# Output units of a feed-forward layer: quarter results subtracted on VectorE instead of GpSimd, six tiles split in the following stage, and a table of angles built in five parts

## The chip, the cores and the metric

One NeuronCore of a Trainium2 chip runs the whole program as a single launch. The metric is device time in microseconds (us). The core has five engines with a queue each: TensorE for matrix products (PE in the profile; PEld is its loading of stationary operands), VectorE (DVE), ScalarE (ACT), GpSimd (POOL) and SyncE (SP), which here only issues DMAs. Each engine works through its own queue in order; engines wait for one another through semaphores.

## What is computed

A trunk of two layers over 512 tokens and a width of 1024, all in float32. Layer 0 mixes tokens with a Conformer convolution module, layer 1 with a sparse attention (NSA). Each is followed by a SwiGLU feed-forward layer with 2816 hidden units:

```python
def swiglu_ffn(h, w_in, w_out):
    gate, up = jnp.split(h @ w_in, 2, axis=-1)
    return (jax.nn.silu(gate) * up) @ w_out

for i in range(DEPTH):
    h = rmsnorm(x, norm_mix[i])
    x = x + (conformer_conv_module(h, ...) if i == 0 else nsa_attention(h, positions, ...))
    h = rmsnorm(x, norm_ffn[i])
    x = x + swiglu_ffn(h, ffn_w_in[i], ffn_w_out[i])
```

The attention rotates part of each query and key by an angle that depends on the position; the kernel needs the cosines and sines of these angles as two tables.

## The kernel before

The residual x lies transposed in eight tiles x[0] to x[7] of 128 channels by 512 tokens. Every operand of a product is split into a rounded part and a remainder (`wh`, `wl` for weights, `hh`, `hl` for the normed x, `sh`, `sl` for sums of weights): ScalarE writes the rounded part, VectorE subtracts it from the value to get the remainder, and TensorE makes three matmuls in place of one (high by high, high by low, low by high).

The program runs through these stages in order of time: convolution module, feed-forward layer 0, attention, feed-forward layer 1. The end of a feed-forward layer (function `ffn`, from line 801) is what the change is about. It multiplies the hidden units by `w_out` in two ways:

- **Row stage.** Fourteen of the 22 hidden blocks are taken one at a time (the loop over `j` with `start(j)`, lines 1090 to 1106). Each row is 24 matmuls of 512 columns into eight PSUM banks. At each row ScalarE and VectorE also split the weights of the next row (`w_hi`, `w_lo`) and the hidden block of a later one (`row_part`, by the table `ROW_AT`). Beside that, in rows 2 to 6 they prepare the operands of the next stage: `raw_blocks` splits three quarter-blocks of two hidden tiles and then forms four differences and sums of quarters in place, with `nc.gpsimd.tensor_tensor` (line 1059); `sum_blocks` splits those. In layer 0, row 7 also calls `between()`, which builds the whole angle table (`rope_tables`, line 1190): a DMA of the positions, ten VectorE operations, three ScalarE operations, two more on VectorE. At the end the eight banks are added to x.
- **Output units.** The other eight hidden blocks go through four units (`out_pair`, line 1131), each of which gives two output tiles m0 and m1 by a scheme with seven products of half-size blocks in place of eight. A product is 12 matmuls of 256 columns (four chunks of the contraction, three matmuls each). TensorE's order in a unit is: weights (into bank a), part ga (bank d), the previous unit's last product (`out_tail`), ga again (a), weights again (b), gb (d), gb (a). Copies of intermediate results (c1, c5, c2) are made by ScalarE; `take_half` subtracts such a copy from a half of an x tile on GpSimd, `add_half` adds a PSUM bank to a half on VectorE. GpSimd also forms the sums of weights that the next unit needs (`s_add`, two operations) and issues the DMAs `s_pre` and `s_acc`; `s_part` (in `s_g1`, `s_g2` and for gc) splits these sums.

When an x tile of layer 0 is complete, `give` calls `finish_x`: `split_x` makes `hh[m]` (ScalarE) and `hl[m]` (VectorE) for the attention's projections, and `sum_x` squares the tile on ScalarE and adds it to the accumulator `acc` of the RMS norm, on VectorE for odd m and on GpSimd for even m. In a unit this stands between `add_half(m0, 1, ...)` and `add_half(m1, 1, ...)`. In layer 1 there is no next stage and `give` stores the tile to the output instead.

The attention begins with `proj_start` (line 395): eight steps k, each with 12 matmuls of 512 columns that use `hh[k]` and `hl[k]`. Functions hooked to a step are called behind it; before, `norm_1` (sum over channels by TensorE, then a reciprocal square root on VectorE) stands behind step 2, `norm_2` (broadcast by TensorE, copy by ScalarE) behind step 3.

The order of the work is written by hand: instructions wrapped in `pe(...)` or `held(...)`, and all of them while `order[0]` is true, keep their place in the program order of their engine. Others are placed by the compiler's scheduler. Nearly all instructions go through the wrapper `Ordered`, so the profile gives line 149 for them; they are told apart by the names of their tiles.

Of the kernel before, what the change touches and what calls it, by code (L numbers as in the profile page):

```python
# [19 lines left out]
P = 128  # L20
T = 512
# [49 lines left out]

QV_ORDER = (0, 1, 2, 3, 4, 5, 6, 7, 8, 9)
VW = (304, 256)
NSA_HOOKS = ("", "", "a", "b", "", "", "", "lc")
BESIDE = {
# [34 lines left out]
NR = len(RROWS)  # L110
NOUT = NK // 2
NALL = NST + NOUT
ROW_SLOT = {11: "gah", 12: "gal", 13: "S2", 14: "gbh", 15: "gah", 16: "gal", 17: "S2", 18: "gbh", 19: "S2", 20: "gbh", 21: "gbl"}
ROW_AT = {1: (21, 11), 2: (12,), 3: (13,), 4: (14,), 5: (15,), 6: (16,), 7: (17,), 8: (18,), 10: (19,), 11: (20,)}
RAW_AT = {2: 0, 3: 1, 4: 2, 5: 3}
SUM_AT = {3: 0, 4: 1, 5: 2, 6: 3}
TABLES_AT = 7
ROW_ORDER = {0: (0, 1, 2, 3, 4), NR - 1: (0, 1, 2, 7, 5, 6, 3, 4)}
OUT_N = 256
EDGE = 24  # L120
# [41 lines left out]
def trunk(ctx: ExitStack, tc: tile.TileContext, A, out):  # L162
# [11 lines left out]
    def nm(s):  # L174
        cnt[0] += 1
        return f"{s}_{cnt[0]}"
# [186 lines left out]
    def finish_x(m, gcol, acc, eng=None):  # L363
        split_x(m, gcol)
        sum_x(m, acc, eng)
# [435 lines left out]
    def ffn(acc, gnext, layer, between=None):  # L801
# [9 lines left out]
        with ExitStack() as cx:  # L811
# [96 lines left out]
            def s_add(n):  # L908
                if n < NALL:
                    w = raws[u0 + n + (NR if n >= NST else 0)]  # L910
                    t = S2[n] = sw.tile([P, 2 * T], F32, tag="S2", name=nm("S2"))
                    pe(nc.gpsimd.tensor_tensor(t[:, :T], S[n][:, :T], w[:, :T], ALU.add))
                    pe(nc.gpsimd.tensor_tensor(t[:, T:], t[:, :T], w[:, T:2 * T], ALU.add))
# [120 lines left out]
                rh[f] = ah[f], al[f]  # L1034

            def row_part(f):
                t = sw.tile([P, 2 * T], F32R, tag=ROW_SLOT[f], name=nm("row"))
                rh[f] = h_, l_ = t[:, :T], t[:, T:]
# [12 lines left out]
            def raw_blocks(c):  # L1051
                y1, y2 = ys[SROWS[c]], ys[SROWS[c + 4]]
                block(c, slice(0, H), y1[:, :H], True)
                block(c, slice(H, 3 * H), y2)
                for z, a, b, o in ((y1[:, :H], y1[:, :H], y1[:, H:], ALU.subtract),
                                   (y1[:, H:], y1[:, H:], y2[:, H:], ALU.subtract),
                                   (y2[:, H:], y1[:, :H], y2[:, H:], ALU.add),
                                   (y2[:, :H], y2[:, :H], y2[:, H:], ALU.subtract)):
                    pe(nc.gpsimd.tensor_tensor(z, a, b, o))

            def sum_blocks(c):
                block(c, slice(3 * H, 5 * H), ys[SROWS[c]])
                block(c, slice(5 * H, 7 * H), ys[SROWS[c + 4]])
# [26 lines left out]
            for j in range(1, NR):  # L1090
                start(j)
                for f in ROW_AT.get(j, ()):
                    row_part(f)
                if j in RAW_AT:
                    raw_blocks(RAW_AT[j])
                if j in SUM_AT:
                    sum_blocks(SUM_AT[j])
                if j == NR - 2:
                    s_add(NST)
                if j == NR - 1:  # L1100
                    s_g1(NST)
                if j == TABLES_AT and layer == 0:
                    hold[0], order[0] = False, True
                    between()
                    hold[0], order[0] = True, False
                row_mm(j, ROW_ORDER.get(j, range(NK)))
            for m in ROW_ORDER[NR - 1]:
# [6 lines left out]

            def take_half(m, h, t):
                z = x[m][:, h * H:(h + 1) * H]
                pe(nc.gpsimd.tensor_tensor(z, z, t, ALU.subtract))

            def give(m, h=None):
                if gnext is None:  # L1120
                    c = slice(0, T) if h is None else slice(h * H, (h + 1) * H)
                    nc.sync.dma_start(out[m][:, c], x[m][:, c])
                elif h is None:
                    hold[0], order[0] = False, True
                    finish_x(m, gnext, acc, nc.vector if m % 2 else nc.gpsimd)
                    hold[0], order[0] = True, False

            def out_tail(q):
# [2 lines left out]
            def out_pair(n, prev):  # L1131
                m0 = 2 * (n - NST)
                m1 = m0 + 1
                end = n == NALL - 1
                q = dict(n=n, a=bank(), m1=m1)
                w1 = next_w(False)
                product(q["a"], w1, 0, 0, True, True)
                s_g2(n)
                s_acc(n + 2)
                s_pre(n + 3)  # L1140
                s_add(n + 1)
                s_load(n + 2)
# [12 lines left out]
                s_part(n, "gc", raw[n])  # L1155
                b = bank()
                product(b, w1, 1, 1, True, True)
                take_half(m0, 1, copied(q["a"], "c2"))
                s_g1(n + 1)
                if end:  # L1160
                    product(q["a"], part[n, "gb"], 0, 4, False, True)
                    add_half(m1, 1, q["a"])
                    give(m1, 1)
                product(q["d"], part[n, "gb"], 1, 2, False, True)
                add_half(m0, 0, b)
                if end:
                    give(m0, 0)
# [3 lines left out]
                if end and gnext is None:  # L1171
                    give(m0, 1)
# [8 lines left out]
                q = out_pair(n, q)  # L1181
            out_tail(q)
            add_half(q["m1"], 0, q["a"])
            give(q["m1"], 0) if gnext is None else give(q["m1"])
            hold[0] = False
            sx.close()
        return acc
# [2 lines left out]
    def rope_tables():  # L1190
        rp = hx[0].enter_context(tc.tile_pool(name="rp", bufs=1))
        cosT = rp.tile([P, T], F32, name="cosT")
        sinT = rp.tile([P, T], F32, name="sinT")
        pos = tp.tile([P, T], I32, tag="sq", name="pos")
        nc.gpsimd.dma_start(pos, A["positions"].partition_broadcast(P))
        pf = tp.tile([P, T], F32, tag="sq", name="posf")
        n = tp.tile([P, T], F32, tag="sq", name="ropen")
        g = nc.vector
        g.tensor_copy(pf, pos)
        g.tensor_scalar(pf, pf, v(V_INVF), None, ALU.mult)  # L1200
        big = 1.5 * 2.0 ** 23
        g.tensor_scalar(n, pf, 1.0 / (2.0 * math.pi), big, ALU.mult, ALU.add)
        g.tensor_scalar(n, n, -big, None, ALU.add)
        for c in _two_pi_pieces():
            g.scalar_tensor_tensor(pf, n, -c, pf, ALU.mult, ALU.add)
        lim = 3.1415925
        g.tensor_scalar(pf, pf, lim, -lim, ALU.min, ALU.max)
        nc.scalar.activation(sinT, pf, AF.Sin)
        nc.scalar.activation(n, pf, AF.Abs)
        nc.scalar.activation(cosT, n, AF.Sin, bias=halfpi, scale=-1.0)  # L1210
        g.tensor_scalar(sinT, sinT, v(V_SGN), None, ALU.mult)
        g.tensor_scalar(cosT, cosT, v(V_ISR), v(V_NISR), ALU.mult, ALU.add)
        return cosT, sinT


    def nsa(acc, cosT, sinT, gnext):
# [112 lines left out]
            box["R"] = norm_b(box["r"], p2, "p2")  # L1329

        def nsa_hooks():
            f = {"l": loads, "c": C["split"], "a": norm_1, "b": norm_2}
            hs = {}
# [614 lines left out]
    acc = conv_module()  # L1948
    cx0.close()
    rope = []  # L1950
    acc = ffn(acc, V_NM1, 0, lambda: rope.extend(rope_tables()))
    cosT, sinT = rope
    acc = nsa(acc, cosT, sinT, V_NF1)
    ffn(acc, None, 1)
    hx[0].close()
# [164 lines left out]
```

## Time and profile before

| | |
|---|---|
| median of 3 runs | 1193.58 us (1193.27 to 1194.09) |
| the profiled execution, its own time | 1193.79 us |
| its span, first to last instruction | 1192.0 us |
| mean granted TensorE clock | 0.997 |
| busy: PE, DVE, ACT, POOL | 1166.9, 870.8, 589.2, 459.9 us |
| row stage of layer 0, output units of layer 0 | about 412 to 485 us, 485 to 535 us of the span |
| start of the attention's projections | from 535 us |
| output units of layer 1 | 1149 us to the end |

The page gives the busy time of each engine and groups instructions by line, operation and tiles. A row of the timeline has the start in us, the duration, the engine, the operation with output tile and input tiles, the count, and in square brackets the idle time before it and what ended it. A row of a group has the count, the busy time in us, the mean of one instruction in ns, and idle time before it with what ended it. A row of the windows has, for a stretch of the span, the busy time of PE, PEld, DVE, ACT and POOL (with counts), the granted clock of TensorE and DMA figures. Ends of matmuls are modelled, so a short wait between two matmuls can be hidden under the modelled end of the first.

### The profile page before, as it was taken

What the parts mean: (1) busy time and instruction counts of PE and PEld (TensorE: products, weight loads), DVE (VectorE), ACT (ScalarE), POOL (GpSimd) and SP (SyncE); (2) the same over time, 40 slices, a digit from 0 to 9 for tenths busy, and PEclk for the clock granted to TensorE, in tenths of its full rate; (3) what the DMA queues carried; (4) which work ended last, traced back from release to release, by engine and by line L of the source; (5) the groups of instructions that cost most, each with busy time, mean ns of one, the idle gap of its engine ahead of it and who ended that gap; (6) DMA issues with size and microseconds to landing.
All of it is one profiled execution on the core that took longest, in us unless ns stands there. A gap on an engine that the chain in (4) does not pass through costs nothing.

```text
span 1192.0 us, 21615 instructions
## 1 busy us (share of the span) xinstructions
PE 1166.9 (98%) x8303; PEld 1018.2 (85%) x8303; DVE 870.8 (73%) x1526; ACT 589.2 (49%) x1118; POOL 459.9 (39%) x484
## 2 busy tenths in 40 slices
PE   9999899999999999989999999999999999999998
PEld 7888678899999987888778877777888999998888
DVE  7989696878777585784678788774497887766566
ACT  6212363455555452453434688783354555545343
POOL 1039022135444160543222468661303544433245
PEclk9999999999999999999999999999999999999999
DMA  9735326357777522424354211111534877772333
GB/s 365 259 109 143 81 89 194 103 163 203 187 194 203 153 100 93 115 80 117 109 133 123 71 37 37 36 37 56 182 112 129 198 200 189 196 201 89 105 103 94
DMA packets 84440, 160.60 MB, mean 135 GB/s; under 512 B 36336, under 2 KB 37488, under 8 KB 83568
## 3 DMA queue, kind: packets, MB, share of 16 engines
q1 hardware_dynamic: 65664, 106.95, 29.0%
q0 software_dynamic: 18672, 52.27, 18.6%
q8 instruction: 65, 1.06, 0.4%
q14 instruction: 39, 0.32, 0.1%
HBM read 145.66 MB, written 5.28 MB: 127 GB/s over the span
## 4 chain that ended last, share of the span: by engine, by line
PE 51%; DVE 4%; issue 3%; POOL 2%; ACT 2%; DVEq 0%; POOLq 0%; ACTq 0%
PE st L149 23%; PE pp L149 15%; PE O L149 3%; PE S L149 3%; PE T L149 3%; PE pv L149 2%; POOL S L149 1%; DVE sl L149 1%; ACT Pm L149 1%; DVE Pm L149 1%; POOL x L149 1%; DVE x L149 1%; PE psc L149 0%; PE z L149 0%; PE psq L149 0%
## 5 line engine op out<-in xcount | busy, mean ns | idle before, releaser
L149 PE MATMUL st<-ball,sh 128*128 128x256 f32 x1680 | 294.3, 277 | 6.7 <-DVE x L149 6.2
L149 PEld LDWEIGHTS st<-ball,sh 128*128 128x128 f32 x1680 | 255.4, 189 | 8.1 <-DVE x L149 7.3
L149 ACT ACTIVATE wh<-wr 128x1024 fp32r<-128x1024 f32 (+3 forms) x146 | 151.1, 1035 | 205.8 <-PE st L149 72.6
L149 DVE TENSOR_TENSOR wl<-wr,wh 128x1024 fp32r<-128x1024 f32 (+3 forms) x146 | 182.5, 1250 | 79.3 <-ACT wh L149 77.0
L149 PE MATMUL st<-ball,sl 128*128 128x256 f32 x840 | 232.9, 277 | 1.7 <-DVE sl L149 1.7
L149 POOL TENSOR_TENSOR S<-S,wr 128x512 f32<-128x512 f32 x84 | 121.6, 1448 | 140.3 <-PE st L149 58.4
L149 PE MATMUL pp<-hh,wh 128*128 128x512 f32 x416 | 165.4, 398 | 1.7 <-ACT wh L149 1.0
L149 PE MATMUL pp<-hl,wh 128*128 128x512 f32 x416 | 162.2, 390 | 0.0
L149 PE MATMUL pp<-hh,wl 128*128 128x512 f32 x416 | 162.0, 390 | 0.1
L149 PEld LDWEIGHTS st<-ball,sl 128*128 128x128 f32 x840 | 159.1, 189 | 2.3 <-DVE sl L149 2.3
L149 POOL DMA_DIRECT2D S<-fw_x x84 | 74.7, 889 | 208.6 <-DVE sl L149 157.3
L149 DVE TENSOR_TENSOR sl<-S,sh 128x512 fp32r<-128x512 f32 x168 | 118.9, 750 | 29.0 <-ACT sh L149 29.0
L149 PE MATMUL st<-ball,wh 128*128 128x256 f32 x672 | 118.7, 276 | 0.0
L149 PE MATMUL st<-row,wh 128*128 128x512 f32 x352 | 108.5, 389 | 0.9 <-ACT wh L149 0.9
L149 POOL TENSOR_SCALAR Pm<-Pm,sm,gates 128x512 f32<-128x512 f32 (+3 forms) x128 | 83.3, 663 | 55.2 <-DVE sm L149 33.7
L149 PEld LDWEIGHTS st<-ball,wh 128*128 128x128 f32 x672 | 101.7, 188 | 0.3
L149 ACT ACTIVATE sh<-S 128x512 fp32r<-128x512 f32 x168 | 96.0, 620 | 7.8 <-PE st L149 6.9
L149 PEld LDWEIGHTS pp<-hh,wh 128*128 128x128 f32 x416 | 78.2, 188 | 22.6 <-issue 3.7
L149 PEld LDWEIGHTS pp<-hh,wl 128*128 128x128 f32 x416 | 78.1, 188 | 17.2 <-DVE wl L149 0.6
L149 PE MATMUL st<-ball,wl 128*128 128x256 f32 x336 | 92.6, 276 | 0.0
L149 PEld LDWEIGHTS pp<-hl,wh 128*128 128x128 f32 x416 | 78.2, 188 | 15.8 <-issue 0.2
L149 ACT ACTIVATE Pm<-Pm,mx 128x512 f32<-128x512 f32 (+3 forms) x128 | 70.7, 554 | 29.9 <-DVE mx L149 27.1
(263 smaller groups left out, 2207.2 us busy)
## 6 DMA issues: line engine op xcount, KB each, us to landing
S<-fw_x POOLq DMA_DIRECT2D x84, 512.0 KB, 6.0
wr<-fw_in SPq DMA_DIRECT2D x46, 512.0 KB
wr<-fw_or SPq DMA_DIRECT2D x28, 512.0 KB
r<-fw_x SPq DMA_DIRECT2D x42, 256.0 KB
bd<-bands POOLq DMA_DIRECT2D x6, 1280.0 KB, 18.4
wr<-cw_in SPq DMA_DIRECT2D x14, 512.0 KB
wr<-fw_s SPq DMA_DIRECT2D x8, 512.0 KB
wr<-fw_op SPq DMA_DIRECT2D x8, 512.0 KB
```

Source lines behind the costliest of these rows:

```text
L149: z = f(*a, **kw)
```

## The change

Six edits, of which the first four apply to both layers:

1. `take_half` and the four in-place differences of `raw_blocks` run on VectorE instead of GpSimd.
2. `raw_blocks` and `sum_blocks` are spread over rows 2 to 9 instead of 2 to 6, and the hidden blocks use other buffers, so that the first unit's sums can be made one row earlier: `s_add(NST)` behind row 11, `s_g1(NST)` behind row 12, and `s_g2(NST)` behind row 13 instead of inside the first unit.
3. In a unit, `w_hi` and `w_lo` of the next weights move ahead of the previous unit's tail; the copy c5 is taken before, and subtracted after, the additions of the previous unit; `s_g1` of the next unit comes ahead of the subtraction of c2.
4. `give` is cut in two: `store` (layer 1) stays where it was.
5. In layer 0 only x[0] and x[1] are finished in the units (in the second and the third unit, both sums on GpSimd). The tiles x[2] to x[7] are split and squared behind steps 0 to 5 of `proj_start` (`LATE`), whose instructions now all keep program order; `norm_1` moves behind step 5 and `norm_2` behind step 6.
6. The angle table is built in five parts behind rows 8 to 12: load, turns (four VectorE operations), rest (six), sines (three ScalarE operations), scaled (two).

```diff
-NSA_HOOKS = ("", "", "a", "b", "", "", "", "lc")
+NSA_HOOKS = ("2", "3", "4", "5", "6", "7a", "b", "lc")
+LATE = {2: (2, 2), 3: (3, 3, 4), 4: (4, 5), 5: (5, 6), 6: (6, 7), 7: (7,)}
...
-ROW_SLOT = {11: "gah", 12: "gal", 13: "S2", 14: "gbh", 15: "gah", 16: "gal", 17: "S2", 18: "gbh", 19: "S2", 20: "gbh", 21: "gbl"}
-ROW_AT = {1: (21, 11), 2: (12,), 3: (13,), 4: (14,), 5: (15,), 6: (16,), 7: (17,), 8: (18,), 10: (19,), 11: (20,)}
-RAW_AT = {2: 0, 3: 1, 4: 2, 5: 3}
-SUM_AT = {3: 0, 4: 1, 5: 2, 6: 3}
-TABLES_AT = 7
+ROW_SLOT = {11: "gah", 12: "gal", 13: "S2", 14: "gbh", 15: "gbl", 16: "gah", 17: "gal", 18: "S2", 19: "gbh", 20: "gbl"}
+ROW_AT = {1: (21, 11), 2: (12,), 3: (13,), 4: (14,), 5: (15,), 6: (16,), 7: (17,), 8: (18,), 9: (19,), 10: (20,)}
+RAW_AT = {2: 0, 4: 1, 6: 2, 8: 3}
+SUM_AT = {3: 0, 5: 1, 7: 2, 9: 3}
+FINISHED = 2
+TABLES_AT = {8: 0, 9: 1, 10: 2, 11: 3, 12: 4}
...
-                    pe(nc.gpsimd.tensor_tensor(z, a, b, o))
+                    pe(nc.vector.tensor_tensor(z, a, b, o))
...
+                if j == NR - 3:
+                    s_add(NST)
                 if j == NR - 2:
-                    s_add(NST)
+                    s_g1(NST)
                 if j == NR - 1:
-                    s_g1(NST)
-                if j == TABLES_AT and layer == 0:
+                    s_g2(NST)
+                if j in TABLES_AT and layer == 0:
                     hold[0], order[0] = False, True
-                    between()
+                    between(TABLES_AT[j])
...
-                pe(nc.gpsimd.tensor_tensor(z, z, t, ALU.subtract))
+                pe(nc.vector.tensor_tensor(z, z, t, ALU.subtract))
...
-                    finish_x(m, gnext, acc, nc.vector if m % 2 else nc.gpsimd)
+                    finish_x(m, gnext, acc, nc.gpsimd)
...
-                s_g2(n)
+                if n > NST:
+                    s_g2(n)
...
                 take_half(m0, 0, copied(q["a"], "c1"))
+                w_hi(state["next"])
+                w_lo()
                 if prev:
                     out_tail(prev)
-                take_half(m1, 1, copied(q["d"], "c5"))
+                c5 = copied(q["d"], "c5")
                 if prev:
                     add_half(prev["m1"], 0, prev["a"])
-                    give(prev["m1"])
-                w_hi(state["next"])
-                w_lo()
+                    store(prev["m1"])
+                    if n <= NST + FINISHED:
+                        give(n - NST - 1)
+                take_half(m1, 1, c5)
...
-                take_half(m0, 1, copied(q["a"], "c2"))
+                c2 = copied(q["a"], "c2")
                 s_g1(n + 1)
+                take_half(m0, 1, c2)
...
                 add_half(m0, 1, q["d"])
...
                 else:
-                    give(m0)
-                if not end:
+                    store(m0)
                     add_half(m1, 1, q["a"])
...
         def nsa_hooks():
+            def late(m, *sums):
+                split_x(m, V_NM1)
+                for i in sums:
+                    sum_x(i, acc, nc.vector if i % 2 else nc.gpsimd)
...
+        order[0] = True
         pss = proj_start(px, "px", hh, hl, nsa_hooks())
+        order[0] = False
```

`rope_tables` is cut into the five functions `load`, `turns`, `rest`, `sines` and `scaled`, with the same operations in the same order.

More of the change, by code (lines that the diff above doesn't have):

```diff
@@ L1036, in row_part @@
             def row_part(f):
-                t = sw.tile([P, 2 * T], F32R, tag=ROW_SLOT[f], name=nm("row"))
-                rh[f] = h_, l_ = t[:, :T], t[:, T:]
+                if f in ROW_SLOT:
+                    t = sw.tile([P, 2 * T], F32R, tag=ROW_SLOT[f], name=nm("row"))
+                    rh[f] = h_, l_ = t[:, :T], t[:, T:]
+                else:
+                    rh[f] = h_, l_ = [sw.tile([P, T], F32R, tag="gc" + e, name=nm("row")) for e in "hl"]
                 pe(nc.scalar.activation(h_, ys[f], AF.Copy))
@@ L1116, in take_half, with store @@
                 z = x[m][:, h * H:(h + 1) * H]
-                pe(nc.gpsimd.tensor_tensor(z, z, t, ALU.subtract))
-            def give(m, h=None):
+                pe(nc.vector.tensor_tensor(z, z, t, ALU.subtract))
+            def store(m, h=None):
                 if gnext is None:
@@ L1122, in give @@
                     nc.sync.dma_start(out[m][:, c], x[m][:, c])
-                elif h is None:
+            def give(m):
+                if gnext is not None:
                     hold[0], order[0] = False, True
-                    finish_x(m, gnext, acc, nc.vector if m % 2 else nc.gpsimd)
+                    finish_x(m, gnext, acc, nc.gpsimd)
                     hold[0], order[0] = True, False
@@ L1162, in out_pair @@
                     add_half(m1, 1, q["a"])
-                    give(m1, 1)
+                    store(m1, 1)
                 product(q["d"], part[n, "gb"], 1, 2, False, True)
@@ L1166, in out_pair @@
                 if end:
-                    give(m0, 0)
+                    store(m0, 0)
                 else:
@@ L1170, in out_pair @@
                 add_half(m0, 1, q["d"])
-                if end and gnext is None:
-                    give(m0, 1)
-                else:
-                    give(m0)
-                if not end:
+                if end:
+                    store(m0, 1)
+                else:
+                    store(m0)
                     add_half(m1, 1, q["a"])
@@ L1183, in ffn @@
             add_half(q["m1"], 0, q["a"])
-            give(q["m1"], 0) if gnext is None else give(q["m1"])
+            store(q["m1"], 0)
             hold[0] = False
@@ L1193, in rope_tables @@
         sinT = rp.tile([P, T], F32, name="sinT")
[L1194 to L1197, printed above, removed]
         g = nc.vector
[L1199 to L1212, printed above, removed]
@@ L1213, in rope_tables, with load, turns @@
-        return cosT, sinT
+        z = {}
+        def load():
+            z["pos"] = tp.tile([P, T], I32, tag="sq", name="pos")
+            nc.gpsimd.dma_start(z["pos"], A["positions"].partition_broadcast(P))
+        def turns():
+            pf = z["pf"] = tp.tile([P, T], F32, tag="sq", name="posf")
+            n = z["n"] = tp.tile([P, T], F32, tag="sq", name="ropen")
+            g.tensor_copy(pf, z["pos"])
+            g.tensor_scalar(pf, pf, v(V_INVF), None, ALU.mult)
+            big = 1.5 * 2.0 ** 23
+            g.tensor_scalar(n, pf, 1.0 / (2.0 * math.pi), big, ALU.mult, ALU.add)
+            g.tensor_scalar(n, n, -big, None, ALU.add)
@@ new lines, in rest, with sines @@
+        def rest():
+            pf, n = z["pf"], z["n"]
+            for c in _two_pi_pieces():
+                g.scalar_tensor_tensor(pf, n, -c, pf, ALU.mult, ALU.add)
+            lim = 3.1415925
+            g.tensor_scalar(pf, pf, lim, -lim, ALU.min, ALU.max)
+        def sines():
+            pf, n = z["pf"], z["n"]
+            nc.scalar.activation(sinT, pf, AF.Sin)
+            nc.scalar.activation(n, pf, AF.Abs)
+            nc.scalar.activation(cosT, n, AF.Sin, bias=halfpi, scale=-1.0)
@@ L1216, in nsa, with scaled @@
+        def scaled():
+            g.tensor_scalar(sinT, sinT, v(V_SGN), None, ALU.mult)
+            g.tensor_scalar(cosT, cosT, v(V_ISR), v(V_NISR), ALU.mult, ALU.add)
+        return cosT, sinT, (load, turns, rest, sines, scaled)
     def nsa(acc, cosT, sinT, gnext):
@@ L1331, in nsa_hooks @@
         def nsa_hooks():
+            def late(m, *sums):
+                split_x(m, V_NM1)
+                for i in sums:
+                    sum_x(i, acc, nc.vector if i % 2 else nc.gpsimd)
             f = {"l": loads, "c": C["split"], "a": norm_1, "b": norm_2}
+            for k, z in LATE.items():
+                f[str(k)] = lambda z=z: late(*z)
             hs = {}
@@ L1950, in trunk, with tables @@
     rope = []
-    acc = ffn(acc, V_NM1, 0, lambda: rope.extend(rope_tables()))
-    cosT, sinT = rope
+    def tables(i):
+        if not rope:
+            rope.extend(rope_tables())
+        rope[2][i]()
+    acc = ffn(acc, V_NM1, 0, tables)
+    cosT, sinT = rope[:2]
     acc = nsa(acc, cosT, sinT, V_NF1)
```

## The prediction

> **What bounds the kernel now.** I read the page first, then the waits of TensorE, then its timeline and the granted clock at the two ends of feed-forward layers, then the chain of waits there, and last the groups of these stretches.
>
> ```profile
> span 1192.0 us, 21615 instructions
> PE 1166.9 (98%) x8303; PEld 1018.2 (85%) x8303; DVE 870.8 (73%) x1526; ACT 589.2 (49%) x1118; POOL 459.9 (39%) x484
> ```
>
> TensorE is the bound: no edit here removes a matmul, so all that can be won is time in which it waits or runs slowly. In its timeline, the output units of layer 0 run from the first row here to the last:
>
> ```profile
> 485.50 0.39 PE L149 MATMUL st<-ball,wh 128*128 128x256 f32 x2
> ...
> 499.24 0.50 PE L149 MATMUL st<-ball,sh 128*128 128x256 f32 x2 [2.66 <-DVE x L149]
> ...
> 512.31 0.39 PE L149 MATMUL st<-ball,sh 128*128 128x256 f32 x2
> ...
> 516.39 0.39 PE L149 MATMUL st<-ball,sh 128*128 128x256 f32 x2
> ...
> 535.19 0.39 PE L149 MATMUL pp<-hh,wh 128*128 128x512 f32 x1
> ```
>
> Between the third and fourth of them lie 12 groups of three matmuls without a wait: 4.08 us / 36 = 0.1133 us each. Four units of seven products of 12 matmuls are 336, so 38.1 us; they took 535.19 - 485.50 = 49.7. The loss is 11.6 us. Its longest wait, 2.66 us, has this chain of waits ahead of it:
>
> ```profile
> 489.81 1.34 POOL S L149
> ...
> 493.37 3.50 POOL x L149 x3
> ...
> 497.35 0.73 ACT hh L149
> ...
> 498.10 0.75 DVE hl L149
> ```
>
> GpSimd first forms sums of weights, then does three subtractions from x; VectorE's addition to the same half waits for the third; `split_x` of that tile waits for the addition, and VectorE stands still until ScalarE has made `hh`; only behind `hl` comes the addition that frees bank a for TensorE's tail product. After the gap the clock falls:
>
> ```profile
> 500.00:505.00 5.00, 5.00 (x31) 5.00 (x31) 3.41 (x5) 3.48 (x7) 4.39 (x4) 0.66 0.44 80
> 525.00:535.00 10.00, 9.53 (x69) 9.14 (x69) 7.93 (x11) 4.75 (x9) 3.24 (x3) 0.86 0.20 64
> ```
>
> The granted clock is 0.66 over 5 us and 0.86 over 10 us: 5 x 0.34 + 10 x 0.14 = 3.1 us of the 11.6 are slow matmuls behind gaps; the rest is waiting.
>
> **The units of layer 0, part by part.** The groups of this stretch (485.5 to 535.2 us):
>
> ```profile
> L149 POOL TENSOR_TENSOR x<-x,c 128x256 f32<-128x256 f32 x12 | 14.8, 1257 | 3.4 <-ACT c L149 3.4
> L149 DVE TENSOR_TENSOR sl<-S,sh 128x512 fp32r<-128x512 f32 x14 | 12.6, 940 | 0.0
> L149 POOL TENSOR_TENSOR S<-S,wr 128x512 f32<-128x512 f32 x6 | 9.0, 1503 | 4.0 <-DVE sl L149 3.7
> L149 DVE TENSOR_TENSOR wl<-wr,wh 128x1024 fp32r<-128x1024 f32 x5 | 8.4, 1676 | 0.4 <-ACT wh L149 0.3
> L149 DVE TENSOR_TENSOR x<-x,st 128x256 f32<-128x256 f32 x15 | 5.9, 411 | 1.5 <-PE st L149 1.2 <-POOL x L149 0.3
> L149 DVE SCALAR_TENSOR_TENSOR hl<-x,vec,hh 128x512 fp32r<-128x512 f32 x7 | 5.8, 834 | 5.5 <-ACT hh L149 5.5
> L149 DVE TENSOR_TENSOR sl<-r,sh 128x512 fp32r<-128x512 f32 x4 | 5.5, 1365 | 0.0
> L149 DVE TENSOR_TENSOR acc<-acc,sq 128x512 f32<-128x512 f32 x3 | 3.7, 1236 | 0.0
> L149 ACT ACTIVATE sq<-x 128x512 f32<-128x512 f32 x6 | 3.7, 614 | 0.0
> L149 POOL TENSOR_TENSOR acc<-acc,sq 128x512 f32<-128x512 f32 x2 | 2.7, 1326 | 6.9 <-ACT sq L149 6.9
> ```
>
> two VectorE rows at moments when GpSimd did no arithmetic, and the first copy of ScalarE:
>
> ```profile
> 488.25 1.28 DVE L149 TENSOR_TENSOR sl<-S,sh 128x512 fp32r<-128x512 f32 x2
> ...
> 532.08 1.21 DVE L149 TENSOR_TENSOR wl<-wr,wh 128x1024 fp32r<-128x1024 f32 x1
> ```
>
> ```profile
> 487.09 0.39 ACT L149 ACTIVATE c<-st 128x256 f32<-128x256 f32 x1 [3.92 <-PE st L149]
> ```
>
> The copy starts 0.23 us behind the 12 matmuls that it reads (485.50 + 1.36).
>
> Removed from GpSimd per unit: three subtractions at 1.257 = 3.8 us. Added to VectorE: three at the price of the nearest row, `add_half`, 0.411 = 1.2 us; that row reads PSUM and the new ones only SBUF, so I allow up to twice that, 2.5 us, when GpSimd is busy, and nothing below 0.3 each. Removed from VectorE: the splits of six tiles (0.834 each, and 5.5 us of standing for `hh`) and three additions to `acc`.
>
> VectorE's sum for a unit is then four parts ga/gb, one gc, one wl, and seven half tiles. At the undisturbed rows, with gc priced like a part: 5 x 0.64 + 1.21 + 7 x 0.411 = 7.3 us. At the disturbed means: 4 x 0.940 + 1.365 + 1.676 + 7 x 0.411 = 9.7. The two units that also split a tile add 0.8. TensorE's time is 84 x 0.1133 = 9.5. GpSimd keeps only the two sums (2 x 1.503 = 3.0 us of arithmetic in place of 6.8) and once an `acc`. In that proportion I take 7.3 + 2.4 x 3.0 / 6.8 = 8.4, and 9.2 with a split, under TensorE's 9.5.
>
> Deadlines, with 1.36 us a product: the ga parts queue on VectorE behind c2, which ScalarE copies when the fourth product ends (5.4 us); 0.2 and the copy 0.4, two high parts at the price of a square, 1.2, and the last low part, 0.6 to 1.4, give 8 to 9 us, due at 10.9 with the next unit's second product. The addition that frees bank a is now last in the unit with nothing but `add_half` ahead: done 0.2 + 0.4 us after the unit, due at 2.7. `w_lo` ahead of the tail delays only the c5 subtraction, for which nobody waits. So each wait that TensorE now has gets about 2 us of room. In the first unit `s_g2` leaves VectorE's queue, GpSimd's `s_pre` no longer stands behind it, and the sums come a row early. I take 11.0 of the 11.6; bounds 6 and 11.6.
>
> [...]
>
> **Row stage.** ScalarE's `wh` starts when TensorE leaves a row:
>
> ```profile
> 439.94 1.06 ACT L149 ACTIVATE wh<-wr 128x1024 fp32r<-128x1024 f32 x1 [0.93 <-PE st L149]
> 445.38 1.06 ACT L149 ACTIVATE wh<-wr 128x1024 fp32r<-128x1024 f32 x1 [0.31 <-PE st L149]
> ...
> 463.71 1.06 ACT L149 ACTIVATE wh<-wr 128x1024 fp32r<-128x1024 f32 x1 [4.91 <-PE st L149]
> ```
>
> A row is 5.44 us; the next three, with the table in them, took 18.33 instead of 16.32: 2.0 us lost. VectorE's rows show why:
>
> ```profile
> 450.38 3.60 DVE L149 SCALAR_TENSOR_TENSOR posf<-ropen,posf 128x512 f32<-128x512 f32 x5
> ...
> 457.36 1.23 DVE L149 TENSOR_TENSOR wl<-wr,wh 128x1024 fp32r<-128x1024 f32 x1 [0.40 <-ACT wh L149]
> ```
>
> `wl` of row 9 stood in the queue behind the whole table. In parts, the dearest (these five, 3.6, and one more, at most 0.7) shares row 10 with wl 1.23 and a row part, 0.64 like the others of its size: 6.2 us, 0.7 over a row, but the `wl` comes first in each row and rows 11 to 13 hold little. The positions' DMA goes into GpSimd's queue at row 8, where the quarter operations no longer stand. The row of groups for VectorE from 418 to 480 us gives the cover:
>
> ```profile
> L149 DVE TENSOR_TENSOR wl<-wr,wh 128x1024 fp32r<-128x1024 f32 x11 | 15.4, 1400 | 18.3 <-ACT wh L149 18.1
> ```
>
> 18.3 us idle take the 16 new quarter operations, 16 x 0.411 = 6.6 us. Saving 2.0, bounds 0 and 2.0.
>
> **Units of layer 1.** No tile is split there; the first matmul and the last addition:
>
> ```profile
> 1149.17 0.39 PE L149 MATMUL st<-ball,wh 128*128 128x256 f32 x2
> ```
>
> ```profile
> 1188.93 0.42 DVE L149 TENSOR_TENSOR x<-x,st 128x256 f32<-128x256 f32 x1 [0.87 <-PE st L149]
> ```
>
> Without a wait the last addition would start at 1149.17 + 38.1 + 0.2 = 1187.5; it started at 1188.9: 1.4 us to win, bounds 0 and 1.4. The stores behind it are unchanged.
>
> **Attention start.** Four rows of its chain of waits and of VectorE:
>
> ```profile
> 535.36 8.19 PE pp L149 x36
> 543.54 0.79 PE ssq L149 x8
> ```
>
> ```profile
> 544.37 0.16 DVE L149 TENSOR_SCALAR ra<-ssq 128x4 f32<-128x4 f32 x1 [1.37 <-PE ssq L149]
> ...
> 546.55 0.16 DVE L149 SCALAR_TENSOR_TENSOR rsy<-rsy 128x4 f32<-128x4 f32 x1
> ```
>
> A step is 8.19 / 3 = 2.73 us. A late tile adds to it on ScalarE 0.73 + 0.61, beside half a `wh` (1.06); on VectorE 0.83, half a `wl` and, for odd tiles, up to 1.24; on GpSimd, for even tiles, 1.33: about 1.9, 2.2 and 0.7 a step. Tile k is due 2.73 k us after the start. Step 0 and 1 and the idle of each queue hide it; without that cover see the last rival. GpSimd's DMAs of `loads`, now pinned behind its sums, feed small products several tiles later. The pinned norm is tighter: from ssq to the end of the reciprocal root 546.55 + 0.16 - 543.54 = 3.2 us, and step 6 covers 0.8 + 2.7 = 3.5. I charge 0.4, bounds 0 and 3.
>
> **Sum.** 11.0 + 2.0 + 1.4 - 0.4 = 14.0 us off the profiled execution's own 1193.79 (span 1192.0 and 1.8 around it; 0.02% above the median shown): 1179.8.
>
> **Rivals.** *VectorE becomes the bound of the units.* At the disturbed prices it needs 9.7 us a unit, 10.5 with a split, against 9.5: 0.2 x 6 + 1.0 x 2 = 3.2 us, and a clock dip as at 500 us, 1.7: 1179.8 + 4.9 = about 1184.7. For it: wl at 1.676 against 1.21. Against: GpSimd loses half its work. [...] Chance 0.17.
>
> *The dips are not the gaps' doing.* Then 3.1 us stay: 1182.9. Against it: the dip begins right behind the longest gap. Chance 0.05.
>
> *The change doesn't do all it says:* the table still holds a `wl` back: 1181.8. Chance 0.07.
>
> *Slower: the attention start becomes serial.* Its instructions are pinned, the squares have two buffers, and `acc` alternates between GpSimd and VectorE; if ScalarE stands at a square, the weights' `wh` stands behind it. With nothing overlapped a tile costs 0.73 + 0.61 + 0.83 + 1.33 and half of wh and wl, 1.4: 4.9 us, and then 2.73 / 0.66 = 4.1 of slow matmuls; 9.0 - 2.73 = 6.3, six times 38: 1218. It decides from 14 / 6 = 2.3 us a tile. Against it: each queue holds about 2 us a step and runs ahead. Chance 0.05.
>
> **Numbers.** The forecast has 0.66: its own range is 1178.8 (all of 11.6 + 2.0 + 1.4 won) to 1182. With 0.8 us below for the spread of the runs shown, and the first three rivals above, 1178.0 to 1185.5 leaves out the slow case and some of the tails. Under 0.2% (2.4 us, about what a measurement of this kernel can tell from no change) needs five sixths of the gain gone. Faster 0.93, same 0.02, slower 0.05.
>
> **What would show it.** Right: the four units of layer 0 near 38 to 39 us with the clock at 1.00 throughout; three rows around the table in 16.3 us; the first eight steps of the attention still 24 us to the next tile; VectorE at 8 to 9 us a unit. Wrong: TensorE waiting for `sl` or `x` in the units with VectorE without idle time (first rival), a wait for `hl`, `wh` or `rsy` between steps 2 and 7 (the slow one).

## The result and the profile after

The changed kernel takes 1180.24 us (median of 5, 1178.24 to 1180.94) against 1194.09 us before (median of 5): a ratio of 0.9883, 95% interval 0.9868 to 0.9897. The profiled execution is the fastest of the five, 1178.24 us. Its page:

```profile
span 1176.5 us, 21609 instructions
PE 1160.9 (99%) x8303; PEld 1014.1 (86%) x8303; DVE 864.9 (74%) x1581; ACT 589.5 (50%) x1118; POOL 400.6 (34%) x429
```

TensorE has the same 8303 matmuls. Its timeline gives the new ends of the output units (first matmul of the units of layer 0, first of the attention, first of the units of layer 1):

```profile
484.02 0.39 PE L151 MATMUL st<-ball,wh 128*128 128x256 f32 x2
...
522.14 0.39 PE L151 MATMUL pp<-hh,wh 128*128 128x512 f32 x1
```

```profile
1135.08 0.39 PE L151 MATMUL st<-ball,wh 128*128 128x256 f32 x2
```

and VectorE's timeline the start of the last addition:

```profile
1173.40 0.42 DVE L151 TENSOR_TENSOR x<-x,st 128x256 f32<-128x256 f32 x1 [0.94 <-PE st L151]
```

The units of layer 0 take 522.14 - 484.02 = 38.1 us in place of 49.7, which is 336 matmuls back to back; those of layer 1, 38.3 in place of 39.8. Windows over single units (two of layer 0 with a split in them, one of layer 1) show the granted clock (third figure from the end) at 1.00, and VectorE's busy time (the third figure with a count) under TensorE's (the first):

```profile
492.20:501.70 9.50, 9.50 (x86) 9.50 (x85) 8.62 (x14) 5.96 (x11) 3.60 (x2) 1.00 0.42 143
501.70:511.30 9.60, 9.60 (x87) 9.60 (x86) 8.73 (x13) 5.95 (x11) 5.33 (x3) 1.00 0.21 69
1143.20:1152.70 9.50, 9.50 (x87) 9.50 (x86) 8.07 (x13) 4.93 (x9) 3.60 (x2) 1.00 0.30 101
```

In the row stage ScalarE's `wh` rows around the table stand at an even 5.4 us:

```profile
451.40 1.06 ACT L151 ACTIVATE wh<-wr 128x1024 fp32r<-128x1024 f32 x1 [2.87 <-issue]
456.79 1.06 ACT L151 ACTIVATE wh<-wr 128x1024 fp32r<-128x1024 f32 x1 [2.98 <-PE st L151]
462.28 1.06 ACT L151 ACTIVATE wh<-wr 128x1024 fp32r<-128x1024 f32 x1 [2.87 <-issue]
467.67 1.06 ACT L151 ACTIVATE wh<-wr 128x1024 fp32r<-128x1024 f32 x1 [3.81 <-PE st L151]
```

467.67 - 451.40 is 16.27 us for three rows, where three rows took 18.33. Against the stages before, the profiled execution wins 2.0 in the row stage, 11.6 and 1.4 in the units, loses 0.1 at the start of the attention, and differs by two amounts that no edit explains: 0.5 us lost ahead of the row stage and 1.1 won inside the attention, whose code is the same. The stretch from the attention's first `kr` to the next norm took between 297.2 and 299.8 us in the 14 profiled executions of this study, in no order that follows an edit. So below the lengths of the stages are compared first, and medians only beyond that spread.

### The profile page after: what moved, and what is told of

Same layout as the page of the kernel before. It is cut to its first block, busy times and chain, and to the rows that moved or that the text cites. A ratio compares the mean times of both kernels' runs of the same rounds, so it can differ in the third digit from the quotient of the medians.

```text
span 1176.5 us, 21609 instructions
## 1 busy us (share of the span) xinstructions
PE 1160.9 (99%) x8303; PEld 1014.1 (86%) x8303; DVE 864.9 (74%) x1581; ACT 589.5 (50%) x1118; POOL 400.6 (34%) x429
## 4 chain that ended last, share of the span: by engine, by line
PE 94%; DVE 3%; ACT 1%; issue 1%; DMA 0%; SPq 0%; DVEq 0%; ACTq 0%
PE st L151 47%; PE pp L151 29%; PE S L151 4%; PE O L151 4%; PE T L151 3%; PE cpe L151 2%; PE pv L151 2%; DVE c L151 1%; PE psc L151 0%; DVE a L151 0%; ACT wh L151 0%; ACT sh L151 0%; DMA x<-xT 0%; PE lng L151 0%; PE z L151 0%
## 5 line engine op out<-in xcount | busy, mean ns | idle before, releaser
L151 PE MATMUL st<-ball,sh 128*128 128x256 f32 x1680 | 290.2, 275 | 0.0
L151 DVE TENSOR_TENSOR wl<-wr,wh 128x1024 fp32r<-128x1024 f32 (+3 forms) x146 | 178.7, 1224 | 70.5 <-ACT wh L151 70.5
L151 DVE TENSOR_TENSOR sl<-S,sh 128x512 fp32r<-128x512 f32 x168 | 111.6, 706 | 29.7 <-ACT sh L151 29.1
L151 ACT ACTIVATE Pm<-Pm,mx 128x512 f32<-128x512 f32 (+3 forms) x128 | 70.7, 555 | 28.9 <-DVE mx L151 26.0
```

The lines of the kernel that those rows point to most:

```text
L151: z = f(*a, **kw)
```

## The experiments

Each kernel is one or two edits away from the kernel before or from the changed one. "Units" is the length of the four output units by the rows used above, layer 0 and layer 1. takes_only and late_only start from the kernel before; the others start from the changed one and keep its rows (the quarter differences on VectorE and spread out, the table in parts). No run has the early sums with the old order, so what they win without the new order stays open.

| kernel | subtractions | splits | first sums | order in unit | units, us | median, us |
|---|---|---|---|---|---|---|
| before | GpSimd | in units | late | old | 49.7, 39.8 | 1194.1 |
| takes_only | VectorE | in units | late | old | 47.1, 39.0 | 1190.6 |
| late_only | GpSimd | late | late | old | 42.3, 39.8 | 1186.3 |
| splits_takes_back | GpSimd | in units | early | new | 45.3, 38.3 | 1187.0 |
| splits_back | VectorE | in units | early | new | 43.0, 38.3 | 1183.8 |
| splits_behind | VectorE | in units, later | early | new | 42.7, 38.3 | 1183.4 |
| splits_end | VectorE | in units, last | early | new | 40.1, 38.3 | 1181.0 |
| order_only | GpSimd | late | late | new | 40.4, 39.5 | 1183.3 |
| sums_late | VectorE | late | late | new | 38.7, 38.9 | 1180.1 |
| takes_back | GpSimd | late | early | new | 38.1, 38.3 | 1179.3 |
| changed | VectorE | late | early | new | 38.1, 38.3 | 1180.2 |

**takes_only.** The kernel before with the quarter subtractions alone on VectorE.

```diff
-                    pe(nc.gpsimd.tensor_tensor(z, a, b, o))
+                    pe(nc.vector.tensor_tensor(z, a, b, o))
-                pe(nc.gpsimd.tensor_tensor(z, z, t, ALU.subtract))
+                pe(nc.vector.tensor_tensor(z, z, t, ALU.subtract))
```

> The kernel before with one edit: the quarter subtractions (take_half in the units, the four differences of raw_blocks) on VectorE. Theory A (two links: the subtractions and the splits between the additions must both leave the chain to TensorE's tail product): layer 1 gets its whole 1.4 us, layer 0 only part, since the chain addition, hh, hl, addition stays and VectorE has about 11 us of work a unit with two splits in it; units of layer 0 at 43 to 47 us against 49.7 before; in all 4 to 8 us faster than before, 1186 to 1190. Theory C (GpSimd's subtractions alone were the loss): units of layer 0 near 38.1 us, 13 us faster, 1181. [...]

1190.62 us; ratio to before 0.9967, interval 0.9956 to 0.9979. The units of layer 0 win 2.6 us of 11.6 and those of layer 1 0.8 of 1.4. Theory C falls; A's bounds (43 to 47 us, 1186 to 1190) are just missed, and layer 1 did not get its whole 1.4 us as A had it.

**takes_back.** The changed kernel with `take_half`, the subtractions in the units, on GpSimd again (the quarter operations of the row stage stay on VectorE).

```diff
-                pe(nc.vector.tensor_tensor(z, z, t, ALU.subtract))
+                pe(nc.gpsimd.tensor_tensor(z, z, t, ALU.subtract))
```

> The changed kernel with take_half of the units on GpSimd again. Theory A: without splits between the additions the GpSimd chain costs in each layer what it cost in layer 1 before, about 1.4 us, so 2 to 4 us slower than the changed kernel, 1182 to 1184. Theory C: the loss of the units comes back, 11 to 13 us slower, 1192. [...]

1179.25 us (0.9871, interval 0.9857 to 0.9886): not slower than the changed kernel, and the units are as long to the hundredth of a microsecond. Theory A falls here: the edit after which the change is named gains nothing once the others are in. The windows over the units of layer 0 say why, takes_back first, then the changed kernel:

```profile
484.00:522.00 38.00, 38.00 (x336) 38.00 (x336) 31.98 (x42) 22.81 (x41) 23.68 (x19) 1.00 0.33 96
```

```profile
484.00:522.00 38.00, 38.00 (x336) 37.98 (x335) 31.98 (x54) 22.80 (x41) 11.20 (x7) 1.00 0.34 96
```

In each row the third figure with a count is VectorE's busy time and the fifth GpSimd's. GpSimd is relieved of 12.5 us, VectorE takes 12 more instructions, and its busy time is 31.98 us in both. The groups of VectorE show what it paid with while the subtractions were on GpSimd (takes_back, then changed):

```profile
L151 DVE TENSOR_TENSOR sl<-S,sh 128x512 fp32r<-128x512 f32 x12 | 11.4, 985 | 0.1
...
L151 DVE TENSOR_TENSOR sl<-r,sh 128x512 fp32r<-128x512 f32 x4 | 4.4, 1094 | 0.0
```

```profile
L151 DVE TENSOR_TENSOR sl<-S,sh 128x512 fp32r<-128x512 f32 x12 | 7.7, 684 | 0.3
L151 DVE TENSOR_TENSOR x<-x,c 128x256 f32<-128x256 f32 x12 | 6.1, 510 | 0.5 <-ACT c L151 0.5
```

**splits_back.** The changed kernel with every tile finished in the units at the old places, and the attention start's hooks and the engine of the sums to `acc` as before.

```diff
                     store(prev["m1"])
-                    if n <= NST + FINISHED:
-                        give(n - NST - 1)
+                    give(prev["m1"])
                 take_half(m1, 1, c5)
...
                     store(m0)
+                    give(m0)
                     add_half(m1, 1, q["a"])
```

> The changed kernel with all eight tiles finished inside the units at the places where the kernel before had them (one split between the last two additions of a unit, sums on VectorE for odd and GpSimd for even tiles), and the attention start as before. Theory A: units of layer 0 43 to 47 us, 5 to 9 us slower than the changed kernel, 1185 to 1189. Theory B (only VectorE's work per unit counts, about 10 us with two splits against TensorE's 9.5): units about 40 us, 2 us slower, 1182. Theory C: no change, 1180.

1183.8 us (0.9912, interval 0.9897 to 0.9926), units 43.0: 4.9 us of the units' gain belong to the late splits. The units are at the edge of A's range and above B's; the median is below A's 1185.

**splits_behind.** splits_back with each split one place later.

```diff
-                    give(prev["m1"])
                 take_half(m1, 1, c5)
+                if prev:
+                    give(prev["m1"])
...
-                    give(m0)
                     add_half(m1, 1, q["a"])
+                    give(m0)
```

> As splits_back, the same work in the units, but each split one place later: behind the addition that frees bank a, and behind the subtraction of c5. Theory A (the place in the chain costs, not the work): most of the loss of splits_back goes away, units 39 to 42 us, 1181 to 1184. Theory B (the work counts): the same time as splits_back within 1 us.

1183.39 us, units 42.7: as theory B had it, since the units are within 0.3 us of splits_back. (The time would fit A's range too, the length of the units doesn't.) But it isn't only work. TensorE now waits for something else, and ScalarE's timeline has the cause:

```profile
511.71 0.50 PE L151 MATMUL st<-ball,sh 128*128 128x256 f32 x2 [1.64 <-ACT c L151]
```

```profile
509.63 0.72 ACT L151 ACTIVATE hh<-x,vec 128x512 fp32r<-128x512 f32 x1 [3.01 <-DVE x L151]
510.26 0.61 ACT L151 ACTIVATE sq<-x 128x512 f32<-128x512 f32 x1
510.78 0.61 ACT L151 ACTIVATE sh<-r 128x512 fp32r<-128x512 f32 x1
511.30 0.36 ACT L151 ACTIVATE c<-st 128x256 f32<-128x256 f32 x1
```

ScalarE stands 3 us at `hh`, which needs VectorE's addition to that tile; the copy c2, which must be taken before TensorE can go on in its bank, stands behind it in the queue. The wait had moved from one engine's queue to another's.

**splits_end.** Both splits of a unit behind everything else in it (splits_back is the kernel compared with; the tiles of the last two units follow behind the tail).

```diff
                     store(prev["m1"])
-                    give(prev["m1"])
                 take_half(m1, 1, c5)
...
                     store(m0)
-                    give(m0)
                     add_half(m1, 1, q["a"])
+                    if prev:
+                        give(prev["m1"])
+                    give(m0)
```

> All splits inside the units as in splits_back, but both of a unit at its very end, behind the addition that frees bank a: on ScalarE hh then stands behind the unit's copies c1, c5, c2 and the high parts of the next sums. In splits_behind TensorE waited 3.7 us for a copy c that stood in ScalarE's queue behind an hh, which waited for a VectorE addition. Theory H (the place in ScalarE's and VectorE's queues costs): units 38 to 40 us, within 1.5 us of the changed kernel. Theory G (the work costs: VectorE needs about 10 us a unit with two splits and two sums, TensorE 9.5): units 41 to 43 us, 3 us slower, as splits_behind.

1180.97 us, units 40.1. So of the 4.9 us, 2.9 were the place in the queues (theory H), and 2.0 remain, less than the 3 us of theory G. Two windows, from the start of the third unit and on to the end, and TensorE's two longest waits:

```profile
501.10:511.50 10.40, 10.40 (x94) 10.40 (x93) 10.19 (x13) 6.93 (x13) 5.28 (x3) 1.00 0.10 26
511.50:523.40 11.90, 10.56 (x90) 10.16 (x90) 10.86 (x20) 7.67 (x14) 4.35 (x1) 1.00 0.27 90
```

```profile
515.46 0.50 PE L151 MATMUL st<-ball,sh 128*128 128x256 f32 x2 [0.58 <-ACT c L151]
...
521.97 0.51 PE L151 MATMUL st<-ball,sh 128*128 128x256 f32 x2 [0.76 <-DVE x L151]
```

VectorE is busy 10.19 of 10.40 us and TensorE does not wait there; both waits come in the last unit and its tail, one for a copy of ScalarE and one for VectorE. That VectorE is at the end of its time (theory G) fits this, but how much of the 2.0 us is its work and how much again a place in a queue was not tried. With their splits placed last, the six tiles would have cost 2 us in the units.

**late_only.** The kernel before with the late splits alone: `give` finishes only tiles 0 and 1, at the old places, and `proj_start` has the hooks of the change.

```diff
-                elif h is None:
+                elif h is None and m < 2:
```

> The kernel before with one edit: only x[0] and x[1] are finished in the units of layer 0, x[2] to x[7] behind steps 0 to 5 of the attention's projections, with the norm behind steps 5 and 6; the subtractions stay on GpSimd, sums, order and table as before. The changed kernel with the subtractions on GpSimd again was as fast as the changed kernel, so theory A (both must go) has fallen. Theory E (the splits in the units are the main cost): units of layer 0 like layer 1's before, 39.8 us, plus under 1 us; 9 to 10 us faster than before, 1185. Theory F (splits, order of the unit and early sums each hold a part): units 42 to 45 us, 5 to 8 us faster, 1187 to 1190.

1186.33 us (0.9935, interval 0.9918 to 0.9952): 7.4 us in the units of layer 0, nothing in layer 1. Theory E had the size of the kernel's time nearly, F the length of the units; the splits are the largest part but not the main cost alone. This run shows a second thing, below.

**splits_takes_back.** splits_back with `take_half` on GpSimd, so that of the change in the units only the early sums and the order are left.

```diff
-                pe(nc.vector.tensor_tensor(z, z, t, ALU.subtract))
+                pe(nc.gpsimd.tensor_tensor(z, z, t, ALU.subtract))
```

> splits_back (all splits inside the units at the old places) with take_half on GpSimd too: of the change, the early sums, the new order in the unit and the table in parts remain. Theory G (VectorE's work per unit is the limit while the splits are there): VectorE loses 1.2 us a unit, so faster than splits_back or equal, units 41 to 43 us, 1182 to 1184. Theory A in what is left of it (with splits in the units the GpSimd chain counts): units 45 to 48 us, 1186 to 1190.

1186.99 us, units 45.3 and 38.3: A's place, not G's. With the splits in the units the subtractions on GpSimd do cost 2.3 us in layer 0; in layer 1, without splits, nothing.

**sums_late.** The changed kernel with the first sums where they were.

```diff
-                if j == NR - 3:
+                if j == NR - 2:
                     s_add(NST)
-                if j == NR - 2:
+                if j == NR - 1:
                     s_g1(NST)
-                if j == NR - 1:
-                    s_g2(NST)
...
-                if n > NST:
-                    s_g2(n)
+                s_g2(n)
```

> The changed kernel with the first unit's sums at the places of before: s_add behind row 12, s_g1 behind row 13, s_g2 inside the first unit. Theory A: the first unit has 2 us of room without them; VectorE takes the two gb parts (1.3 us) in the first unit and GpSimd's next sums start behind them, so 0 to 1.5 us slower, 1180 to 1181.7. Theory F (early sums hold a part of the gain that the splits don't): 2 to 4 us slower.

1180.11 us; units 38.7 and 38.9, 0.6 us longer in each layer, within theory A's 0 to 1.5 us.

**order_only.** sums_late and takes_back together: to the diff above comes

```diff
-                pe(nc.vector.tensor_tensor(z, z, t, ALU.subtract))
+                pe(nc.gpsimd.tensor_tensor(z, z, t, ALU.subtract))
```

> The changed kernel with take_half on GpSimd again and the first unit's sums at the places of before (late splits, new order in the unit and table in parts remain). Each of the two alone cost nothing much: 1179.3 with the subtractions back, 1180.1 with the sums late. Theory J (GpSimd's queue: with late sums its DMA s_pre waits for VectorE's gb part, its next sums start 6 us later, and the subtractions pile up behind them; either edit alone dissolves the pile): units of layer 1 at 39.5 to 39.8 us again and of layer 0 at 40 to 42.5, so 3 to 6 us slower than the changed kernel, 1183 to 1186. Theory K (the new order in the unit did it, neither of the two is needed once it is there): units at 38.1 to 38.9 us in both layers, 1180 to 1181.

1183.28 us (0.9911, interval 0.9897 to 0.9926); units 40.4 and 39.5. Each of the two edits alone gives up at most 0.6 us a layer, both together 2.3 and 1.1: theory J, and K falls. GpSimd's timeline at the first unit shows the pile:

```profile
487.84 0.57 POOL L151 DMA_DIRECT2D S<-fw_x  x1 [15.28 <-DVE sl L151]
488.42 3.74 POOL L151 TENSOR_TENSOR S<-S,wr 128x512 f32<-128x512 f32 x2
492.12 3.05 POOL L151 TENSOR_TENSOR x<-x,c 128x256 f32<-128x256 f32 x3
```

The DMA of `s_pre` waits for the buffer that VectorE's gb part still reads; the sums and all three subtractions of the unit stand behind it, and TensorE then waits for an addition of VectorE that needs these subtractions. Layer 1 has the same pile. TensorE's rows of the two layers, and the DMA in layer 1:

```profile
496.01 0.51 PE L151 MATMUL st<-ball,sh 128*128 128x256 f32 x2 [0.83 <-DVE x L151]
...
1150.42 0.50 PE L151 MATMUL st<-ball,sh 128*128 128x256 f32 x2 [0.83 <-DVE x L151]
```

```profile
1142.26 0.58 POOL L151 DMA_DIRECT2D S<-fw_x  x1 [14.75 <-DVE sl L151]
```

In takes_back the same queue runs freely:

```profile
481.47 0.57 POOL L151 DMA_DIRECT2D S<-fw_x  x1 [9.30 <-DVE sl L151]
482.05 2.69 POOL L151 TENSOR_TENSOR S<-S,wr 128x512 f32<-128x512 f32 x2
485.77 0.75 POOL L151 TENSOR_TENSOR x<-x,c 128x256 f32<-128x256 f32 x1 [1.03 <-ACT c L151]
```

There the first subtraction waits only for its copy c1, and TensorE has no such wait in the units of either layer.

**table_once.** The changed kernel with all parts of the table behind row 10.

```diff
-TABLES_AT = {8: 0, 9: 1, 10: 2, 11: 3, 12: 4}
+TABLES_AT = {10: 0}
-                    between(TABLES_AT[j])
+                    for i in range(5):
+                        between(i)
```

> The changed kernel with all five parts of the angle table behind row 10. Theory A: wl of row 12 stands behind the whole table and TensorE loses about 2.0 us in the row stage as before; 1182.2. If ScalarE's and VectorE's idle time in rows 11 to 13 is cover enough, no change, 1180.2.

1183.67 us. From the third `wh` of the row stage to the units it takes 70.7 us, against 65.3 in the changed kernel and 67.3 before: 5.4 us lost in place of the 2.0 expected. TensorE's two waits, VectorE's row, GpSimd's row and a window:

```profile
475.25 0.73 PE L151 MATMUL st<-row,wh 128*128 128x512 f32 x2 [2.70 <-ACT wh L151]
476.51 0.50 PE L151 MATMUL st<-row,wl 128*128 128x512 f32 x1 [0.53 <-DVE wl L151]
```

```profile
466.26 5.59 DVE L151 SCALAR_TENSOR_TENSOR posf<-ropen,posf 128x512 f32<-128x512 f32 x5
```

```profile
467.60 2.98 POOL L151 TENSOR_TENSOR S<-S,wr 128x512 f32<-128x512 f32 x2 [51.29 <-DMA wr<-fw_op]
```

```profile
476.00:481.00 5.00, 4.49 (x13) 3.58 (x14) 2.79 (x4) 1.19 (x3) 0.00 (x0) 0.66 0.54 186
```

2.0 us are put down to the old loss of the whole table. The five operations that took 3.6 us before take 5.59 here, 2.0 more, and GpSimd's first sums (the second row), which are a row earlier in this kernel, lie in their time. Behind the wait of 2.70 us the clock is at 0.66 for 5 us (the window): 5 x 0.34 = 1.7 us. Together 5.7 for 5.4 measured. That the sums slow these operations was not tried by itself, nor was another row for the whole table. What is shown is that in the profiled executions the parts are worth 5.4 us of the row stage in the changed kernel, against 2.0 in the kernel before; the medians of table_once and the changed kernel differ by 3.4.

**extra_2 and extra_10.** The changed kernel with 2 or 10 operations of VectorE added to each unit, which change nothing (`range(10)` in the second kernel).

```diff
                 take_half(m1, 1, c5)
+                for _ in range(2):
+                    pe(nc.vector.tensor_tensor(c5, c5, c5, ALU.max))
```

> The changed kernel with two more VectorE operations in each unit, behind the subtraction of c5 (maximum of the copy c5 with itself, 128x256, 0.41 us each, 0.75 together; the result isn't used). VectorE was busy for 8.1 us a unit in layer 1 and 8.7 us in the fullest units of layer 0, TensorE for 9.5. Theory A (about 2 us of room and 0.8 to 1.4 us a unit to spare): no change, within 0.5 us of the changed kernel. First rival of the prediction (VectorE is at its limit): up to 0.75 us a unit, 3 to 6 us slower.

1179.9 us; units 38.3 and 38.3. VectorE was not at its limit.

> As extra_2 with ten operations, 3.5 us a unit, so that VectorE needs 11.6 us in a unit of layer 1 and 12.2 in the fullest of layer 0. Theory A: over three units VectorE falls behind by 2.1 to 2.7 us each, less 2 us of room, in each layer: units about 42 to 44 us in both layers, 8 to 11 us slower than the changed kernel, 1188 to 1191. If the work is not the limit even then, under 3 us slower. On the clock: gaps of 1 to 2 us between products; a dip behind each of them if a gap of that size is what makes the clock fall, none or one if it takes more.

1201.77 us (1.0068 of before, interval 1.0053 to 1.0083); units 51.7 and 48.2. The direction is theory A's and the size isn't. Each of the ten operations, which all read and write the same copy, took 0.45 us in layer 0, and rows of ten took 4.56 to 5.55 us in layer 1, so a unit holds 4.5 us or more of them and not 3.5. TensorE then waits for VectorE from the second unit on, and the window over a unit of layer 1 shows VectorE busy for nearly all of it:

```profile
1159.00:1171.70 12.70, 10.14 (x84) 9.75 (x84) 12.36 (x24) 5.92 (x11) 3.91 (x2) 1.00 0.19 65
```

The clock falls as well, in both layers: it is 0.50 from 509 to 514 us behind a wait of 2.93 us and 0.66 from 524 to 529 behind one of 1.79. From 1174.8 to 1179.9 us three matmuls take 0.64 us, as they do from 509 to 514, where they take 0.34 at a clock of 1.00; that is behind these two waits of layer 1:

```profile
1172.25 0.38 PE L151 MATMUL st<-ball,sl 128*128 128x256 f32 x1 [2.20 <-DVE sl L151]
...
1174.18 0.80 PE L151 MATMUL st<-ball,sh 128*128 128x256 f32 x2 [0.49 <-DVE x L151]
```

## Why the prediction was right

**The sum.** 14.0 us were forecast and the medians differ by 13.9. The three terms by stage are 11.6 (11.0 taken), 2.0 (2.0) and 1.4 (1.4). The attention start was charged 0.4 and cost 0.1, so the stages hold 14.9, and that the medians agree to 0.1 is luck within the spread of the attention. At its start the chain of waits and VectorE's timeline have the pinned norm in time:

```profile
522.30 16.35 PE pp L151 x72
538.65 0.79 PE ssq L151 x8
539.43 2.89 PE pp L151 x12
542.32 0.89 PE rbc L151 x8
```

```profile
541.64 0.16 DVE L151 SCALAR_TENSOR_TENSOR rsy<-rsy 128x4 f32<-128x4 f32 x1
```

The reciprocal root is done at 541.80 and step 6 ends at 542.32: 0.5 us of room where 0.35 was worked out. The six late tiles hide, as their prices against a step of 2.73 us had it.

**VectorE's time.** 8.4 us a unit and 9.2 with a split were taken; 8.07 and 8.6 to 8.7 were measured, with a subtraction at 0.51 us where 0.411 was priced and up to twice that allowed. The room of about 2 us held against two extra operations and not against ten.

**What was wrong in it.** The step "Removed from GpSimd per unit: three subtractions at 1.257 = 3.8 us. Added to VectorE: three ... 1.2 us" stands first among what was to free TensorE, beside the late splits. takes_back shows that it isn't needed once the rest is in, and that VectorE isn't any busier for it: with GpSimd still doing the subtractions VectorE did not become the bound. With the subtractions on GpSimd, it is the early sums that take the chain of layer 1 apart (39.5 us in order_only, 38.3 in takes_back), because the sums and the subtractions no longer stand behind the waiting `s_pre`: the prediction had that clause ("GpSimd's `s_pre` no longer stands behind it") and gave it no price. The subtractions on VectorE and the early sums each dissolve the same pile, which is why either can be undone alone (sums_late 0.6 us a layer, takes_back none) and not both (order_only). Alone in the kernel before, the subtractions on VectorE win only part of it in layer 1 (takes_only, 39.0). In layer 0 the parts overlap too: starting from the kernel before, early sums and order win 4.4 us, then the subtractions 2.3, then the late splits 4.9; in another order the late splits win 7.4 first, the new order in the unit (with the rest of the changed kernel's rows) 1.9, the early sums 2.3 and the subtractions nothing.

**The first rival** (VectorE the bound) is false for the changed kernel and true for extra_10; it fits the 2.0 us of splits_end, where it was not shown. VectorE was busy for 31.98 us of 38.00 with the subtractions on either engine (takes_back and the changed kernel). That bears on the gain of one edit and not on the whole.

**The second rival** (the dips of the clock have another cause than the gaps) was given 0.05 because the dip begins behind the longest gap. In the profiled execution the 3.1 us did go with the gaps. But late_only keeps the same gap and has no dip, which the windows set side by side, before and then late_only:

```profile
494.00:499.00 5.00, 2.58 (x23) 2.38 (x21) 3.92 (x6) 1.65 (x3) 4.01 (x4) 1.00 0.56 163
499.00:504.00 5.00, 4.76 (x27) 4.76 (x28) 3.41 (x6) 3.48 (x8) 3.39 (x3) 0.66 0.57 103
```

```profile
494.00:499.00 5.00, 2.39 (x22) 2.19 (x20) 3.92 (x7) 1.84 (x4) 3.83 (x4) 1.00 0.60 167
499.00:504.00 5.00, 4.95 (x43) 4.95 (x44) 3.70 (x5) 3.77 (x8) 3.58 (x3) 1.00 0.59 98
```

late_only's wait in TensorE's timeline is as long as the one shown of before, 2.66 us:

```profile
499.05 0.50 PE L150 MATMUL st<-ball,sh 128*128 128x256 f32 x2 [2.66 <-DVE x L150]
```

So a gap of this length can bring the dip and need not; the 3.1 us were rightly placed as a loss behind gaps and wrongly as a loss that each such gap brings. Nor is it shown that the whole 3.1 us can be won by the clock alone: of the executions of the kernel before that ran beside the experiments, the two with a mean clock of 1.000 took 1193.43 and 1195.30 us, and the 16 with 0.997 took 1193.10 to 1195.80.

**The table**, in parts, held no `wl` back, so the third rival is false.

## What to carry to other kernels

When a stage loses time to a chain across several in-order queues, list every link that has to be late for the wait to exist: several edits may each break it, and their gains then don't add, so undo each alone and two together before crediting one. Ask of an instruction that waits on another engine what stands behind it in its own queue; moving it only pays if nothing urgent does. Compare by the length of the stage where the kernel has another stage that varies by more than the effect.

## What the runs showed of the hardware

- Work moved from GpSimd to VectorE added nothing to VectorE's busy time, 31.98 us from 484 to 522 us in takes_back and in the changed kernel. The twelve subtractions took 6.1 us there, and VectorE's sixteen `sl` 5.4 us less: means of 985 and 1094 ns with the subtractions on GpSimd, 684 and 680 without. VectorE's additions to a half from a PSUM bank took 413 and 414 ns in the two. One case is to be seen in the changed kernel itself, on VectorE and then on GpSimd:

```profile
508.02 1.53 DVE L151 TENSOR_TENSOR x<-x,c 128x256 f32<-128x256 f32 x1
```

```profile
507.51 1.76 POOL L151 TENSOR_TENSOR acc<-acc,sq 128x512 f32<-128x512 f32 x1
```

  An operation of 0.42 us (the median of the twelve) took 1.53 and ended 0.28 us behind GpSimd's. What held it, no run shows by itself.
- The clock fell (to 0.66 over 5 us in the kernel before and in table_once, to 0.50 over 5 us and 0.66 over another 5 in extra_10) behind single waits of 2.66 us (before) and 2.93 (extra_10), and behind 2.70 (table_once), 2.20 (by the pace of its matmuls) and 1.79 (extra_10) and 1.69 (before) with a wait of about 0.5 or 0.6 us within 3 us of each. It did not behind 2.66 in late_only, nor behind 2.10 in splits_behind (1.00 from 513.5 to 526.8 us), and behind 2.22 and 2.18 in splits_takes_back three matmuls went on taking 0.34 to 0.36 us. So between 1.7 and 2.7 us the length of a wait did not decide by itself; what did is open.
